# First pair's reads between its substitution's steps, three gate and three value buffers, and keys behind the corner transposition

## The chip, the cores and the metric

The kernel runs on one core of a Trainium2 chip. The metric is device time in microseconds (us). Three runs of the kernel before are shown, and their median is 1071.92 us. The engines are named as in the profile: PE multiplies matrices (PEld is its weight load), DVE is the vector engine, ACT the scalar engine, POOL a third elementwise engine, and SP issues nearly all DMAs, in order.

## The reference

One layer of a decoder trunk over 512 positions and 2048 channels, in float32:

```python
h = rms_norm(x, norm_g[i])
z = jnp.einsum('btd,dn->btn', h, w_in[i])          # 2048 -> 6272 columns
... token shift on r, k, v and two low-rank inputs
decay = jnp.exp(-jnp.exp(w_loglog)); a = jax.nn.sigmoid(a0[i] + ad @ a_up[i])
kk = kk / jnp.maximum(jnp.linalg.norm(kk, axis=-1, keepdims=True), KK_EPS)
def step(S, inp):                                  # 16 heads of 64, 512 steps
    sa = jnp.einsum('bhvk,bhk->bhv', S, -kk_t)
    S = S * w_t[:, :, None, :] + sa[..., None] * (kk_t * a_t)[:, :, None, :] + v_t[..., None] * k_t[:, :, None, :]
    return S, jnp.einsum('bhvk,bhk->bhv', S, r_t)
y_rwkv = (head_group_norm(y, ln_w[i], ln_b[i]) + bonus) * jax.nn.silu(g_rwkv)
y_pool = per-group linear map of (trailing means - token), scaled, * jax.nn.silu(g_pool)
x = x + jnp.einsum('btc,cd->btd', concat(y_rwkv, y_pool), w_out[i])
x = x + sigmoid(x @ w_pg[i] + b_pg[i]) * (p[i] @ w_ple[i])
return rms_norm(x, final_g)
```

## The kernel before

Every large product runs as three matmuls: each float32 operand is split into a high part (a cast on ACT, line 133 for weights) and a low part (a subtraction on DVE, line 134), and high·high, high·low and low·high are summed in PSUM (`mm3`). Weights come in chunks of 256 KB (`wsplit`): `raw` is loaded by SP, `whi` and `wlo` are made from it, and each of the three has four buffers. `chunk` asks for weights some six chunks ahead of their use.

The work on the 16 heads goes in eight pairs (`j` from 0 to 7), 128 channels each. The recurrence is worked out in chunks of 64 positions. For each pair:

- `prepare` makes the decayed queries `ar` and the keys `bk` (line 615 the half without the norm, line 619 the half with it), and stores `bk` to memory (`bkd`).
- `scores` multiplies them (`pm`), masks the result into `mt`, stores a part of it (`nd`), and reads it back as the factor of a triangular system, in two halves of four DMAs (`n_read(0)` and `n_read(1)`, line 682). The list `later` holds what else is to be read: the second half, the next pair's low-rank weights (`load_ab`, line 355), and the keys in blocks (`bg`, line 693, twice two DMAs).
- `invert` solves the system by substitution in 31 steps, two DVE instructions each (lines 719 and 723). The first 16 steps read the first half of the factor, the others the second. The result `xw` goes through memory (`xd`, line 727) to `x1` (line 734).
- `gather` transposes the corner block of `x1` (`y1`, line 789) and feeds it to PE (`pq2`, then `px2`) to complete the inverse. For the first two pairs the norm of the next pair's keys (line 572, `late`) is ordered ahead of that transposition. `turn_key` (line 639) transposes the keys that were read.
- `recur` goes over the eight chunks of positions, with the next pair's `scores` and `invert` between its hops; `finish`, `turn_out` and `gate_out` (lines 960 to 985) store the pair's output during the next pair, where line 979 adds the bonus and line 980 multiplies by the gate.

Between all this the kernel puts the projection's matmuls (`pump(n)` puts n of them; `stream` lists the column blocks: for each pair k, r, v, one or more blocks of the pool half, and the gate g). Their results are `sk`, `sr`, `sv` and `sg`; a gate is made from PSUM on ACT (line 374) and DVE (line 375). `psA`, their accumulators, has two buffers.

PE's instructions stay in program order in this part (`keep_in_program_order`). For the other engines the framework lays out an order before the run: it takes the earliest instruction in the program whose inputs and buffers it estimates to be ready. `tc.issue_after(i)` puts instructions behind `i` on its engine, and `tc.high_priority` ahead of others. On the chip each engine's order is fixed.

For the pairs from the second on, the entries of `later` wait in the list `portions`, and `recur` takes one out after each hop. For the first pair, which has no `recur` ahead of it, they were issued all at once behind `n_read(0)`:

```python
for fn in later if j == 0 else ():
    with tc.issue_after(n_.ins):
        fn()
portions[:] = [(n_, fn) for fn in later] if j else []
```

The first pair's substitution was driven by `for _ in invert(0): pump(4)`, that is 124 matmuls beside 31 steps.

Of the kernel before, what the change touches and what calls it, by code (L numbers as in the profile page):

```python
# [9 lines left out]
F32 = mybir.dt.float32  # L10
# [5 lines left out]
P = 128  # L16
# [18 lines left out]
def trunk_kernel(ctx: ExitStack, tc: tile.TileContext, x, p, norm_g, w_in, mu, w0, w_up, a0, a_up,  # L35
# [426 lines left out]
    def stream():  # L462
        for kind, nm, j in jobs:
            if kind == "b":
                yield from pool_unit(j)
                continue
            if kind == "e":
                yield from embed_unit(j)
                continue
            if kind == "p":  # L470
                for k in range(2):
                    pt = rw.tile([P, T], F32, name=f"ppt{k}", tag=("kk", "kp")[k])
                    nc.vector.transpose(pt.rearrange("p (b k) -> p b k", k=32), pn[0][:, k])
                    a_ = rw.tile([P, T], F32R, name=f"phi{k}", tag=("sk", "sr")[k], bufs=2)
                    b_ = rw.tile([P, T], F32R, name=f"plo{k}", tag=("sv", "sg")[k], bufs=(4, 2)[k])
                    split(a_, b_, pt)
                    phl.append((a_, b_))
                yield 3
                continue
            ps = psA.tile([P, T], F32, name=f"z{nm}{j}", tag="acc")  # L480
            yield from zcols(ps, f"{nm}{j}")
            t_ = rw.tile([P, T], F32, name=f"s{nm}{j}", tag=f"s{nm}", bufs=4 if nm == "v" else 2)
            if nm == "g":
                silu2(ps, t_)
            else:
                shifted(ps, t_, {"r": 0, "k": 8, "v": 16}[nm] + j)
            zt[nm, j] = t_
# [24 lines left out]
                assert (nm, j) in zt  # L512
        return zt[nm, j]

    pws, kks, nrs, vgs, late = {}, {}, {}, {}, [None]

    H1, H2, H3, H4, H5, HE = 6, 12, 20, 8, 13, 40

# [79 lines left out]
    def prepare(j):  # L598
        k_, r_, v_ = need("k", j), need("r", j), need("v", j)
        pw, ipw, tha = pws.pop(j)  # L600
        kk = kks.pop(j)


        ar = rw.tile([P, NCH // 2, 4, C], F32, name=f"ar{j}", tag="ar", bufs=2)
        bk = rw.tile([P, NCH // 2, 4, C], F32, name=f"bk{j}", tag="bk")
        k4 = kk.rearrange("p (q c t) -> p q c t", c=2, t=C)
        pw4 = pw.rearrange("p (q c) t -> p q c t", c=2)
        i4 = ipw.rearrange("p (q c) t -> p q c t", c=2)
        kp = rw.tile([P, T], F32, name=f"kp{j}", tag="kp")
        nc.vector.tensor_scalar(kp, tha, dp(33, j), dp(41, j), ALU.mult, ALU.add)  # L610
        nc.vector.tensor_tensor(kp, kp, k_, ALU.mult)
        nc.vector.tensor_scalar(tha, tha, 0.5, 0.5, ALU.mult, ALU.add)
        nc.vector.tensor_tensor(ar[:, :, 0::3, :], r_.rearrange("p (q c t) -> p q c t", c=2, t=C),
                                pw4[:, :, :, 1:C + 1], ALU.mult)
        nc.vector.tensor_tensor(bk[:, :, 0::3, :], kp.rearrange("p (q c t) -> p q c t", c=2, t=C), i4, ALU.mult)
        nc.vector.scalar_tensor_tensor(ar[:, :, 1:3, :], k_.rearrange("p (q c t) -> p q c t", c=2, t=C), dp(89, j),
                                       pw4[:, :, :, 0:C], ALU.mult, ALU.mult)
        nc.vector.tensor_tensor(kk, kk, tha, ALU.mult)
        made = nc.vector.tensor_tensor(bk[:, :, 1:3, :], k4, i4, ALU.mult)
        with tc.issue_after(made.ins):  # L620
            nc.vector.scalar_tensor_tensor(kp, r_, dp(49, j), kp, ALU.mult, ALU.mult)
        kph = rw.tile([P, T], F32R, name=f"kph{j}", tag="t", bufs=4)
        kpl = rw.tile([P, T], F32R, name=f"kpl{j}", tag="t", bufs=4)
        split(kph, kpl, kp)

        if j:
            vd = dram.tile([P, T], F32, name=f"vd{j}", tag="vd")
            with tc.issue_after(read[-1].ins):
                nc.sync.dma_start(out=vd, in_=v_)
            vgs[j] = rw.tile([P, NT, 4, 32], F32, name=f"vg{j}", tag="t", bufs=4), vd  # L630
        bkd = dram.tile([P, NCH * P], F32, name=f"bkd{j}", tag="bkd")
        nc.sync.dma_start(out=bkd, in_=bk.rearrange("p q s c -> p (q s c)"))
        st_[j] = dict(pw=pw, ar=ar, bk=bk, bkd=bkd, v_=v_, kp=(kph, kpl))
# [8 lines left out]
    def scores(j):  # L642
        ar, bk, v_ = (st_[j][n_] for n_ in ("ar", "bk", "v_"))
        kph, kpl = st_[j].pop("kp")

        mt = rw.tile([P, 2, 8, 2, C], F32, name=f"mt{j}", tag="mt", bufs=2)
        pm = [[psM.tile([P, T], F32, name=f"pm{j}_{par}0", tag="m"),
               psY.tile([P, T], F32, name=f"pm{j}_{par}1", tag="y")] for par in range(2)]
        for par in range(2):
            for q in range(4):  # L650
                for h in range(2):
                    rows = slice(64 * h, 64 * h + 64)
                    mm(pm[par][h][:, q * P:(q + 1) * P], bk[rows, q, 2 * par:2 * par + 2, :],
                       ar[rows, q, 2 * par:2 * par + 2, :], start=True, stop=True)
        for par in range(2):
            for h in range(2):
                nc.vector.tensor_tensor(mt[:, par, h::2, :, :],
                                        pm[par][h].rearrange("p (u a t) -> p u a t", u=4, a=2),
                                        msk[:, par:par + 2, :].unsqueeze(1).to_broadcast([P, 4, 2, C]), ALU.mult)


        ps = psM.tile([P, T], F32, name=f"pbo{j}", tag="m")
        mm(ps, blk, kph, start=True, stop=False)
        mm(ps, blk, kpl, start=False, stop=True)
        bv = v_ if j else rw.tile([P, T], F32, name=f"bv{j}", tag="sv", bufs=4)
        nc.vector.tensor_tensor(bv, ps, v_, ALU.mult)

        nd = dram.tile([2, 2, 8, 32, 32], F32, name=f"nd{j}", tag="nd")
        for par in range(2):
            pb = 64 * (1 - par)  # L670
            for b in range(2):
                rows = slice(pb + 32 * b, pb + 32 * b + 32)
                nc.sync.dma_start(out=nd[par, b].rearrange("u r c -> r u c"),
                                  in_=mt[rows, par, :, 1 - par, 32 * b:32 * b + 32])
        nb = []
        for i in range(2):
            t_ = rw.tile([P, 16, 32], F32, name=f"n32{j}_{i}", tag=("kk", "kp")[i])
            nb.append(t_)

        def n_read(i):  # L680
            for q in range(4):
                r_ = nc.sync.dma_start(out=nb[i][32 * q:32 * q + 32], in_=nd[:, :, :, 16 * i:16 * i + 16, :].rearrange(
                    "a b u r c -> (a b u) r c"))
            return r_

        n_ = n_read(0)
        if j:
            hold[:] = [n_]
        bg = rw.tile([P, NCH, 4, 32], F32, name=f"bg{j}", tag="bk")

        def blocks(dst, src, qs):
            for q in qs:
                nc.sync.dma_start(out=dst[32 * q:32 * q + 32],
                                  in_=src.rearrange("(b k) (c q i) -> q k c b i", b=4, q=4, i=32)[q])

        later = [lambda: n_read(1)]
        if j + 1 < NJ:
            later.append(lambda: load_ab(j + 1))
        for qs in ((0, 1), (2, 3)):
            later.append(lambda qs=qs: blocks(bg, st_[j]["bkd"], qs))  # L700
        if j:
            vg, vd = vgs[j]
            for qs in ((0, 1), (2, 3)):
                later.append(lambda qs=qs: blocks(vg, vd, qs))
        for fn in later if j == 0 else ():
            with tc.issue_after(n_.ins):
                fn()
        portions[:] = [(n_, fn) for fn in later] if j else []
        st_[j].update(mt=mt, nb=nb, bv=bv, bg=bg)


# [30 lines left out]
    def gather(j):  # L742
# [44 lines left out]

        with tc.issue_after(late[0].ins):
            yt = nc.vector.transpose(y1, x1[:, :, 0:32])
        with tc.issue_after(yt.ins):  # L790
            if normed:
                normed.pop()()
                stores.pop()()
            if j + 1 < NJ:
                scale_key(j + 1)
# [27 lines left out]
        if gates:  # L823
            gates.append(gates.pop()())


    def recur(j, work, between):
        d = st_.pop(j)
# [16 lines left out]
        for ch in range(NCH):  # L845
# [67 lines left out]
                        yr = slice(64 * pr, 64 * pr + 64)  # L913
                        nc.scalar.copy(ysb[yr, c0 // 2:c0 // 2 + 2, :], py4[yr, pr::2, :])
            step()
            if portions:
                n_, fn = portions.pop(0)
                with tc.issue_after(n_.ins):
                    fn()
            if ch == 1 and gates:  # L920
                with tc.issue_after(lead[0].ins):
                    gates.pop()()
# [77 lines left out]
    pump(H3)  # L1000
    scores(0)
    pump(H2)
    for _ in invert(0):
        pump(4)
    pump(HT - 124)
    gather(0)
# [319 lines left out]
```

## Time and profile before

| | |
|---|---|
| three runs | 1071.4, 1072.0 and 1071.92 us |
| the profiled execution | 1071.41 us, span 1069.7 us |
| granted clock of PE, mean | 0.995 |
| PE busy | 1042.4 us (97%) |
| DVE busy | 713.2 us (67%) |
| ACT busy | 433.5 us (41%) |

The span is the time from the first to the last instruction, and the run's time includes what lies around it. The pairs take the stretch from about 60 to 690 us. Times in the views are us from the span's start; a row of a time line has start, duration, engine, line, operation, output and inputs, and in brackets how long the engine had been idle and what ended that.

### The profile page before, as it was taken

The numbers are of one execution on the slowest core, as the hardware profiler recorded it, in microseconds if no ns is written. First come the engines' busy times: TensorE is split into PE (matmuls) and PEld (weight loads), VectorE is DVE, ScalarE is ACT, GpSimd is POOL, SyncE is SP. The second block draws the span as 40 slices with busy tenths as digits, with TensorE's granted clock in tenths as the row PEclk, the third lists the DMA queues.
The fourth block names the chain that finished last, engine by engine and source line by source line (L and its number), as shares of the span: only waits on it lengthen the run. The fifth ranks groups of instructions, "written<-read, shape, count | busy, mean of one in ns | idle before, by whom it ended". The sixth has DMA issues, their size and how long they took to land.

```text
span 1069.7 us, 17217 instructions
## 1 busy us (share of the span) xinstructions
PE 1042.4 (97%) x5884; PEld 862.0 (81%) x5884; DVE 713.2 (67%) x1878; ACT 433.5 (41%) x893; POOL 75.7 (7%) x180
## 2 busy tenths in 40 slices
PE   5998999999999999999999999999999999999996
PEld 4886888888888888887888888888888888888885
DVE  6677768978788788797787868454444344436356
ACT  7633424434334344353343345543222232323337
POOL 2100011010110110201101101000000000000000
PEclk9999999999999999999999999999999999999998
DMA  7444443553544645535446454774847659455434
GB/s 238 106 120 97 130 126 92 149 146 95 159 117 129 171 103 149 139 93 155 115 118 181 106 139 132 252 233 160 202 143 178 166 149 262 133 185 169 158 99 157
DMA packets 292174, 159.08 MB, mean 149 GB/s; under 512 B 130306, under 2 KB 254827, under 8 KB 292087
## 3 DMA queue, kind: packets, MB, share of 16 engines
q1 hardware_dynamic: 264070, 129.41, 44.3%
q10 hardware_dynamic: 28016, 28.58, 8.8%
q8 instruction: 46, 0.75, 0.3%
q14 instruction: 42, 0.34, 0.1%
HBM read 130.63 MB, written 26.79 MB: 147 GB/s over the span
## 4 chain that ended last, share of the span: by engine, by line
PE 93%; DVE 3%; ACT 2%; DMA 1%; issue 1%; SPq 0%; ACTq 0%; DVEq 0%
PE acc_o L161 16%; PE acc_g L161 16%; PE zb L161 16%; PE zv L161 8%; PE zg L161 8%; PE zr L161 8%; PE zk L161 7%; PE pple L161 2%; PE py L161 2%; PE pu L161 2%; PE pm L161 1%; PE ps L161 1%; PE pp L161 1%; PE pmv L161 1%; PE zl L161 1%; ACT hhi L287 1%
## 5 line engine op out<-in xcount | busy, mean ns | idle before, releaser
L134 DVE TENSOR_TENSOR wlo_g<-raw_g,whi_g 128x512 fp32r<-128x512 f32 x84 | 57.2, 688 | 81.7 <-ACT whi_g L133 81.6
L161 PE MATMUL zb<-hhi,whi_b 128*128 128x512 f32 x256 | 105.1, 411 | 0.0
L161 PE MATMUL zb<-hhi,wlo_b 128*128 128x512 f32 x256 | 100.3, 392 | 0.0
L161 PE MATMUL zb<-hlo,whi_b 128*128 128x512 f32 x256 | 99.8, 390 | 0.0
L161 PE MATMUL acc_o<-wlo_o,yhi 128*128 128x512 f32 x256 | 99.6, 389 | 0.0
L161 PE MATMUL acc_o<-whi_o,ylo 128*128 128x512 f32 x256 | 99.6, 389 | 0.0
L134 DVE TENSOR_TENSOR wlo_o<-raw_o,whi_o 128x512 fp32r<-128x512 f32 x64 | 43.8, 690 | 80.3 <-ACT whi_o L133 80.1
L133 ACT CAST whi_g<-raw_g 128x512 fp32r<-128x512 f32 x84 | 51.8, 619 | 106.9 <-PE acc_g L161 52.6
L161 PE MATMUL acc_o<-whi_o,yhi 128*128 128x512 f32 x256 | 94.7, 389 | 0.0
L161 PE MATMUL acc_g<-whi_g,x2hi 128*128 128x512 f32 x208 | 81.2, 390 | 0.0
L161 PE MATMUL acc_g<-wlo_g,x2hi 128*128 128x512 f32 x208 | 80.9, 389 | 0.0
L899 POOL TENSOR_SCALAR s0p<-sbd,pw 64x64 f32<-64x64 f32 x96 | 57.8, 602 | 325.1 <-DVE sbd L892 247.0
L161 PE MATMUL acc_g<-whi_g,x2lo 128*128 128x512 f32 x208 | 80.7, 390 | 0.0
L133 ACT CAST whi_o<-raw_o 128x512 fp32r<-128x512 f32 x64 | 39.5, 621 | 95.2 <-PE acc_o L161 58.3
L133 ACT CAST whi_b<-raw_b 128x512 fp32r<-128x512 f32 x64 | 39.5, 620 | 55.3 <-PE zv L161 17.5
L134 DVE TENSOR_TENSOR wlo_b<-raw_b,whi_b 128x512 fp32r<-128x512 f32 x64 | 43.9, 688 | 22.9 <-ACT whi_b L133 22.1
L161 PEld LDWEIGHTS zb<-hhi,wlo_b 128*128 128x128 f32 x256 | 48.0, 188 | 10.8
L723 DVE TENSOR_TENSOR xw<-xw,tm 128x60 f32<-128x60 f32 (+24 forms) x248 | 52.1, 210 | 6.8
L161 PEld LDWEIGHTS acc_o<-wlo_o,yhi 128*128 128x128 f32 x256 | 48.1, 188 | 10.1
L161 PEld LDWEIGHTS acc_o<-whi_o,yhi 128*128 128x128 f32 x256 | 48.0, 188 | 10.0
L161 PEld LDWEIGHTS acc_o<-whi_o,ylo 128*128 128x128 f32 x256 | 48.0, 188 | 9.9
L161 PE MATMUL zr<-hhi,whi_r 128*128 128x512 f32 x128 | 53.9, 421 | 1.3 <-DVE sg L375 1.3
(293 smaller groups left out, 2490.0 us busy)
## 6 DMA issues: line engine op xcount, KB each, us to landing
raw_b<-in_w_in_dram SPq DMA_DIRECT2D x64, 256.0 KB
raw_o<-in_w_out_dram SPq DMA_DIRECT2D x64, 256.0 KB
raw_g<-in_w_pg_dram SPq DMA_DIRECT2D x64, 256.0 KB
raw_k<-in_w_in_dram SPq DMA_DIRECT2D x32, 256.0 KB
raw_r<-in_w_in_dram SPq DMA_DIRECT2D x32, 256.0 KB
raw_v<-in_w_in_dram SPq DMA_DIRECT2D x32, 256.0 KB
raw_g<-in_w_in_dram SPq DMA_DIRECT2D x32, 256.0 KB
bkd<-bk SPq DMA_DIRECT2D x8, 512.0 KB
```

Of the source, the lines that this page charges most:

```text
L133: made.append(nc.scalar.copy(hi, raw))
L134: made.append(nc.vector.tensor_tensor(lo, raw, hi.bitcast(F32), ALU.subtract))
L161: i = nc.tensor.matmul(*a, **k)
L287: nc.scalar.activation(hhi[:, d, hc], pt[:, 0:256], AF.Copy, scale=ngc[:, d:d + 1])
L723: nc.vector.tensor_tensor(xw[:, 0:n_, s + 1:32], xw[:, 0:n_, s + 1:32], tm[:, 0:n_, 0:w_], ALU.add)
L899: nc.gpsimd.tensor_scalar(s0p[hc, :], nxt[hc, hc], pcn[hc], None, ALU.mult)
```

## The change

Four edits. The first pair's reads go into the same list `portions` as those of the later pairs, and `next_read` takes one out behind the 3rd, 7th, 11th and 14th step of its substitution (`s` is 2, 6, 10 and 13); the order behind `n_read(0)` stays. The gates `sg` get three buffers in place of two, and the values `sv` three in place of four; the two tiles of the embedding (`plo`) that share these buffers follow. The first key product of a pair (line 615) is ordered behind the corner transposition of the pair before it; the first pair has none.

```diff
-                    b_ = rw.tile([P, T], F32R, name=f"plo{k}", tag=("sv", "sg")[k], bufs=(4, 2)[k])
+                    b_ = rw.tile([P, T], F32R, name=f"plo{k}", tag=("sv", "sg")[k], bufs=3)
...
-            t_ = rw.tile([P, T], F32, name=f"s{nm}{j}", tag=f"s{nm}", bufs=4 if nm == "v" else 2)
+            t_ = rw.tile([P, T], F32, name=f"s{nm}{j}", tag=f"s{nm}", bufs=3 if nm in "vg" else 2)
...
-        nc.vector.tensor_tensor(bk[:, :, 0::3, :], kp.rearrange("p (q c t) -> p q c t", c=2, t=C), i4, ALU.mult)
+        with tc.issue_after(corner[0].ins) if corner else ExitStack():
+            nc.vector.tensor_tensor(bk[:, :, 0::3, :], kp.rearrange("p (q c t) -> p q c t", c=2, t=C), i4, ALU.mult)
...
-        bv = v_ if j else rw.tile([P, T], F32, name=f"bv{j}", tag="sv", bufs=4)
+        bv = v_ if j else rw.tile([P, T], F32, name=f"bv{j}", tag="sv", bufs=3)
...
-        for fn in later if j == 0 else ():
-            with tc.issue_after(n_.ins):
-                fn()
-        portions[:] = [(n_, fn) for fn in later] if j else []
+        portions[:] = [(n_, fn) for fn in later]
...
             yt = nc.vector.transpose(y1, x1[:, :, 0:32])
+        corner[:] = [yt]
...
+    def next_read():
+        if portions:
+            n_, fn = portions.pop(0)
+            with tc.issue_after(n_.ins):
+                fn()
...
-            if portions:
-                n_, fn = portions.pop(0)
-                with tc.issue_after(n_.ins):
-                    fn()
+            next_read()
...
-    for _ in invert(0):
+    for s, _ in enumerate(invert(0)):
+        if s in (2, 6, 10, 13):
+            next_read()
         pump(4)
```

More of the change, by code (lines that the diff above doesn't have):

```diff
@@ L513, in need @@
         return zt[nm, j]
-    pws, kks, nrs, vgs, late = {}, {}, {}, {}, [None]
+    pws, kks, nrs, vgs, late, corner = {}, {}, {}, {}, [None], []
     H1, H2, H3, H4, H5, HE = 6, 12, 20, 8, 13, 40
```

## The prediction

> **What bounds the kernel now.** I began with the page's span and busy lines.
>
> ```profile
> span 1069.7 us, 17217 instructions
> ...
> PE 1042.4 (97%) x5884; PEld 862.0 (81%) x5884; DVE 713.2 (67%) x1878; ACT 433.5 (41%) x893; POOL 75.7 (7%) x180
> ```
>
> TensorE is busy for 97% of the span, so an edit that removes no matmul can win only where PE stands still, or where its clock drops after it stood still. The second view is therefore the waits of PE alone (total us, times, longest), and the third the stretches of 2 us around the longest wait past the start-up.
>
> ```profile
> PE zr L161 <- DVE wlo_r L134: 4.0, 1, 4.0
> ...
> PE zr L161 <- DVE sg L375: 1.3, 1, 1.3
> PE pq L161 <- DVE y L789: 0.8, 1, 0.8
> ...
> PE pu L161 <- DVE zs L859: 0.4, 1, 0.4
> ```
>
> ```profile
> 104.00:106.00 2.00, 0.00 (x0) 0.00 (x0) 1.86 (x7) 0.00 (x0) 0.00 (x0) 1.00 0.00 0
> ...
> 108.00:110.00 2.00, 2.00 (x6) 1.51 (x6) 0.63 (x2) 0.00 (x0) 0.00 (x0) 0.50 0.92 267
> 110.00:112.00 2.00, 2.00 (x8) 1.55 (x7) 0.88 (x2) 1.21 (x2) 0.00 (x0) 0.73 0.91 231
> ```
>
> Past the start-up four waits of PE stand in the list. Three touch what the diff edits: weights during the first pair's substitution, a gate (sg), and the corner transposition (y). The stretches (busy PE, PEld, DVE, ACT, POOL, then PE clock, DMA share, GB/s) add that the longest wait costs more than its 4.0 us: behind it the granted clock is 0.50 and 0.73 in two stretches. The DMA share is zero from 104 to 106, so PE waits for no transfer there, while DVE works 1.86 of 2 us.
>
> **Part 1: the first pair's reads in portions.** The time lines of PE, DVE, ACT and SP (start, duration, engine) tell how the wait comes about.
>
> ```profile
> 98.65 0.39 PE L161 MATMUL zr<-hhi,wlo_r 128*128 128x512 f32 x1
> 102.50 0.39 PE L161 MATMUL zr<-hlo,whi_r 128*128 128x512 f32 x1
> 106.88 0.50 PE L161 MATMUL zr<-hhi,wlo_r 128*128 128x512 f32 x1 [3.99 <-DVE wlo_r L134]
> 111.08 0.39 PE L161 MATMUL zv<-hlo,whi_v 128*128 128x512 f32 x1
> 83.91 0.69 DVE L134 TENSOR_TENSOR wlo_k<-raw_k,whi_k 128x512 fp32r<-128x512 f32 x1 [2.03 <-ACT whi_k L133]
> 104.94 1.31 DVE L639 STREAM_TRANSPOSE bkn<-bg 128x512 f32<-128x512 f32 x2
> 106.17 0.65 DVE L134 TENSOR_TENSOR wlo_r<-raw_r,whi_r 128x512 fp32r<-128x512 f32 x1
> 106.74 1.88 DVE L134 TENSOR_TENSOR wlo_v<-raw_v,whi_v 128x512 fp32r<-128x512 f32 x3
> 98.31 0.62 ACT L133 CAST whi_r<-raw_r 128x512 fp32r<-128x512 f32 x1
> 82.48 3.61 SPq L682 DMA_DIRECT2D n<-nd  x8
> 88.63 3.18 SPq L693 DMA_DIRECT2D bg<-bkd  x4
> 91.91 0.62 SPq L130 DMA_DIRECT2D raw_r<-in_w_in_dram  x1
> ```
>
> The matmul at 106.88 needs the low half of r's fourth weight chunk. Its high half was done on ACT at 98.31 + 0.62 = 98.93, but DVE's order has the low half behind the whole substitution and both key transpositions, which begin where it ends (104.94). The chunk had been loaded late: its buffer was free once wlo_k ended at 83.91 + 0.69 = 84.60, and its load was issued at 91.91, because from 82.48 to 91.81 SP issued the eight reads of the factor, four of the low-rank weights and four of the keys in a row. An order laid out for a chunk that comes late puts its split late.
>
> The price: the 18 rows of zr from 98.65 to 102.50 have 17 spacings, 0.2265 us each. From 102.50 to 111.08 there are 12 spacings, 2.72 us at that pace, and 8.58 passed. The loss is **5.86 us**: 4.15 of standing, and 1.71 at the low clock.
>
> After the edit 12 of these reads go behind steps 2, 6, 10 and 13 of the substitution, so SP can take the r and v loads between. No DMA is added. The next pair's reads go in portions already, with two weight loads between the halves of the factor:
>
> ```profile
> 145.20 1.71 SPq L682 DMA_DIRECT2D n<-nd  x4
> 146.95 0.98 SPq L130 DMA_DIRECT2D raw_k<-in_w_in_dram  x2
> 147.97 1.90 SPq L682 DMA_DIRECT2D n<-nd  x4
> ```
>
> In that pair's substitution PE has no wait for weights in the list above, so I take the whole 5.86 as the gain. Cover: the fourth r load can go some 6 us sooner (about 86 instead of 91.91), which leaves its split 16 us before 102.5.
>
> What is late next? DVE is nearly full in the stretch from 104 above. The four splits at 106.17 and 106.74 (0.65 + 1.88, say 2.5 us) move into the substitution, whose end goes from 104.94 to about 107.4. Behind it hangs the way of its result through memory to the corner transposition y, and from there PE's pq:
>
> ```profile
> 107.45 1.57 SPq L130 DMA_DIRECT2D raw_b<-in_w_in_dram  x3
> 109.07 2.07 SPq L727 DMA_DIRECT2D xd<-xw  x3
> ...
> 120.89 0.43 DVE L789 STREAM_TRANSPOSE y<-x 128x256 f32<-128x256 f32 x1
> 125.77 0.69 PE L161 MATMUL pq<-y,mt 32*32 32x32 f32 x32
> ...
> 470.17 2.53 SPq L727 DMA_DIRECT2D xd<-xw  x4
> 474.63 2.87 SPq L734 DMA_DIRECT2D x<-xd  x4
> ```
>
> PE will want pq at 125.77 − 5.86 = 119.9. Where no weight loads stand between, as at 470.17, the way takes 7.33 us to the last read's issue, and about 1.9 more to land (472.70 to 474.63 is that for the write): 107.4 + 9.3 + 0.43 = 117.1, 2.8 before PE asks. Where loads stand ahead of the stores, as the three at 107.45 do now, y slips by the whole 2.5 and ends at 123.8, and PE waits 3.9, with a clock loss of up to 1.7. So the give-back lies between 0 and 5.6; below nothing it could go by the 0.4 that PE now waits for zs, if a new order heals that. I take **0.4**: the small waits of the seven later pairs (1.3 + 0.8 + 0.4 over 7) are the nearest rows of a pair with portions. The low-rank weights load later too, but nothing reads them before the matmuls that stand behind the whole substitution in PE's order.
>
> What would a remnant at pq cost? The wait of 3.99 lost 1.71 by the clock, 0.43 for each us; in proportion a remnant of 2.5 us would cost 3.6. The Trainium skill, "TensorE: Matmul & The Clock Gate", Part 1, says otherwise: the array falls to half rate only after an idle window of about 3.4 us. By that rule such a remnant costs its own 2.5 us, and the first rival below would give 1066.5 rather than 1067.5. The trace agrees so far: behind the wait of 1.35 at 508 the clock stays at 1.00.
>
> ```profile
> 506.00:510.00 4.00, 2.65 (x13) 2.07 (x12) 3.50 (x8) 1.68 (x3) 0.90 (x2) 1.00 0.90 268
> ```
>
> **Part 2: three gates, three values.** The seventh gate's activation waits for a buffer.
>
> ```profile
> 507.44 0.60 ACT L374 ACTIVATE sg<-zg 128x512 f32<-128x512 f32 x1 [2.72 <-DVE yo L980]
> 508.81 0.50 PE L161 MATMUL zr<-hhi,whi_r 128*128 128x512 f32 x1 [1.35 <-DVE sg L375]
> ...
>   ACT sg L374: 8.0, 3
> ```
>
> With two buffers, gate j+2 waits until gate j is multiplied in at line 980 (8.0 us of ACT in three pairs, by the view of the tile sg); once PE has filled its other accumulator it stands too. A third buffer takes that release away. Gain 1.35 plus the 0.16 by which the first wait's standing exceeded its idle time (4.15 against 3.99): **1.51 us**. The other two waits are beside PE and bring nothing. The values pay with one of four buffers.
>
> ```profile
> 219.52 0.69 DVE L979 TENSOR_TENSOR yo<-yo,bv 128x512 f32<-128x512 f32 x1
> 260.08 0.69 ACT L370 ACTIVATE sv<-zv,dprm 128x512 f32<-128x512 f32 x1
> ```
>
> The first pair's bonus (bv) is last read at 219.52 + 0.69, and the value that with three buffers takes its place (the fourth pair's) is written at 260.08. That cover is 40 us, so the edit costs nothing; without it the value would wait for line 979 as the gate does for 980.
>
> **Part 3: keys behind the corner transposition.**
>
> ```profile
> 481.00 0.68 DVE L615 TENSOR_TENSOR bk<-kp,ipw 128x512 f32<-128x512 f32 x1
> 483.15 0.43 DVE L789 STREAM_TRANSPOSE y<-x 128x256 f32<-128x256 f32 x1
> ```
>
> The key product stands ahead of y on DVE, and this y is the one that PE waits 0.8 for in the list of waits. y's input had been fetched long before (issues end at 474.63 + 2.87 = 477.50), so y comes earlier by what is taken out: at most the 0.68 of that row, of a loss of 0.8 + 0.16 = 0.96. Instructions on DVE start a little before the one ahead has ended (106.17 + 0.65 against 106.74), so I take **0.60**. The wait that is added is on DVE; behind the key product only the store of both halves of the keys is queued, and the other half still waits for its norms, so it costs nothing. If that cover were gone, it would be the same 0.60 on the way to the scores.
>
> **The sum.** 5.86 − 0.4 + 1.51 + 0.60 = 7.57 us. The profiled execution took 1071.41 us (span 1069.7 and 1.7 around it), 0.5 under the median of the runs shown, 1071.92. So it would take 1063.84, and a run of median kind **1064.3 us**.
>
> **The rivals.**
> *The wait moves to pq.* The result of the substitution keeps its place behind weight loads, and PE waits there 1 to 3.9 us. For it: DVE is full and SP is in order. Against it: loads that go out earlier no longer stand between. Gain 7.97 − (1 to 5.6): 1065 to 1069.5.
> *The portions change nothing.* Order on SP and DVE is laid out by estimated readiness; if the fourth r split stays behind line 639, only parts 2 and 3 are left: 1071.92 − 2.1 = 1069.8. Against it: by the rows above it was a late load that put the split there, and nothing else.
>
> ```profile
> 97.23 0.23 DVE L719 TENSOR_TENSOR tm<-xw,n 128x75 f32<-128x75 f32 x1
> ```
>
> *Slower: a portion comes too late.* DVE is in order. If the second factor half or the last keys are queued on SP behind loads that wait for buffers, DVE stands at step 17 or at line 639, with the splits behind it. A wait W there is added to today's stall: 1071.92 − 2.1 + W, slower by 0.2% from W = 4.3. The 17th step, the first to read the second half, begins at 97.23 now, so that half would have to land after 101.5. Against it: its reads are issued by 82.48 + 3.61 = 86.09 now, and would have to slip by a dozen us, past several loads, though their place is behind step 2 of 31. Time at W = 6: 1075.8.
>
> **How the numbers follow.** A measurement of this kernel tells from no change about 0.2%, 2.1 us. Forecast 0.63 (its own range 1062.6 to 1066), moved wait 0.17, no effect of the portions 0.11, late portion 0.09. All of the first two cases but 0.01, and half of the third, are faster: 0.84. Same: 0.08. Slower: 0.08, most of the fourth case. The range reaches from 1062.6 (everything gained, and the 0.4 healed) to 1069.8, the third case.
>
> **What would show it.** Right: no wait of PE for wlo_r, clock 1.00 in every stretch between 100 and 112, raw_r loads between the n and bg reads on SP, no row of ACT sg waiting for line 980, line 615 behind line 789 in every pair but the first. Wrong: a wait of PE at pq near 118, a DVE row of the substitution that waits for nb's or bg's transfer, or new waits for weights in later pairs, where everything is laid out anew.

## The result: 0.6% faster, and the profile after

| | before | after |
|---|---|---|
| median of five runs | 1071.92 us | 1066.03 us |
| range | 1071.4 to 1072.54 | 1065.28 to 1066.23 |
| the profiled execution | 1071.41, span 1069.7 | 1066.03, span 1064.3 |
| granted clock of PE, mean | 0.995 | 0.997 |

The ratio is 0.994, with a 95% interval of 0.9929 to 0.9951. Further down a run stands as such a ratio against runs of the kernel before on the same chip; a few disturbed executions (2120 us and more) are left out of the ratios.

The waits of PE in the changed kernel, those of the start-up left out (total us, times, longest):

```profile
PE pq L161 <- DVE y L787: 1.5, 2, 1.1
PE pu L161 <- DVE zs L864: 0.9, 3, 0.4
```

The waits for wlo_r (4.0) and for the gate sg (1.3) are gone. The wait for y, at 0.8 before, is now 1.5 in two places (0.4 in the first pair, 1.1 in the sixth), and that for zs (a tile of the recurrence), one of 0.4 before, is 0.9 in three. The stretches of 2 us where PE had stood show it busy throughout, at full clock (third number from the end):

```profile
104.00:106.00 2.00, 2.00 (x10) 1.65 (x10) 1.76 (x9) 0.40 (x1) 0.00 (x0) 1.00 0.07 16
108.00:110.00 2.00, 2.00 (x11) 1.65 (x10) 2.00 (x5) 0.62 (x1) 0.00 (x0) 1.00 0.10 16
110.00:112.00 2.00, 2.00 (x13) 1.67 (x12) 0.87 (x3) 1.19 (x2) 0.00 (x0) 1.00 0.73 216
```

The time line of SP in the changed kernel shows what the portions did to the queue:

```profile
82.89 3.61 SPq L683 DMA_DIRECT2D n<-nd  x8
86.54 1.12 SPq L355 DMA_DIRECT2D ur<-in_w_up_dram  x2
87.71 1.23 SPq L355 DMA_DIRECT2D ar<-in_a_up_dram  x2
89.04 0.53 SPq L130 DMA_DIRECT2D raw_r<-in_w_in_dram  x1
89.67 0.45 SPq L130 DMA_DIRECT2D raw_v<-in_w_in_dram  x1
90.22 1.40 SPq L694 DMA_DIRECT2D bg<-bkd  x2
...
110.28 1.87 SPq L725 DMA_DIRECT2D xd<-xw  x3
112.26 2.40 SPq L130 DMA_DIRECT2D raw_g<-in_w_in_dram  x2
114.84 1.85 SPq L732 DMA_DIRECT2D x<-xd  x4
```

In the columns of a time line (start, duration, engine, line, operation, output and input, count), both halves of the factor and the low-rank weights still go out in one row, although in the program they are portions of their own, behind the 3rd and the 7th step. Only the keys (bg) moved behind the fourth r load, which left at 89.04 and not at 91.91. And loads of g still stand between the stores of the substitution's result and its reads.

DVE and ACT answer with another order. The fourth r chunk's high half is made at 94.49 in place of 98.31, and its low half inside the substitution (rows of ACT, then of DVE):

```profile
94.49 0.62 ACT L133 CAST whi_r<-raw_r 128x512 fp32r<-128x512 f32 x1 [1.38 <-PE zk L161]
95.94 0.69 DVE L134 TENSOR_TENSOR wlo_r<-raw_r,whi_r 128x512 fp32r<-128x512 f32 x1
99.33 0.69 DVE L134 TENSOR_TENSOR wlo_v<-raw_v,whi_v 128x512 fp32r<-128x512 f32 x1
107.37 1.29 DVE L640 STREAM_TRANSPOSE bkn<-bg 128x512 f32<-128x512 f32 x2
...
119.50 0.75 DVE L371 SCALAR_TENSOR_TENSOR sv<-zv,prm,sv 128x511 f32<-128x511 f32 x1
120.17 0.44 DVE L787 STREAM_TRANSPOSE y<-x 128x256 f32<-128x256 f32 x1
```

### The profile page after: what moved, and what is told of

Read it like the earlier page. It is cut to its first block, busy times and chain, and to the rows that moved or that the text cites. A ratio compares the mean times of both kernels' runs of the same rounds, so it can differ in the third digit from the quotient of the medians.

```text
span 1064.3 us, 17220 instructions
## 1 busy us (share of the span) xinstructions
PE 1040.8 (98%) x5884; PEld 861.4 (81%) x5884; DVE 714.1 (67%) x1878; ACT 434.0 (41%) x893; POOL 75.6 (7%) x180
## 4 chain that ended last, share of the span: by engine, by line
PE 84%; DVE 3%; issue 1%; ACT 0%; DMA 0%; ACTq 0%; DVEq 0%
PE acc_o L161 16%; PE acc_g L161 16%; PE zb L161 14%; PE zg L161 7%; PE zv L161 6%; PE zr L161 6%; PE zk L161 6%; PE pple L161 2%; PE py L161 2%; PE pu L161 2%; PE pm L161 1%; PE ps L161 1%; PE pp L161 1%; PE pmv L161 1%; DVE sw L418 1%
## 5 line engine op out<-in xcount | busy, mean ns | idle before, releaser
L878 ACT COPY uv<-pu 64x64 f32<-64x64 f32 x128 | 26.3, 205 | 73.4 <-PE pu L161 72.4
```

The source lines that it names most:

```text
L878: u_ = nc.scalar.copy(uv[pb:pb + 64, ch, hc], psu[hc, hc])
```

## The experiments

Four questions: do the edits add up, and which of them pays; was the load of r late, or only DVE's order; what does the low clock cost; and what makes the waits for y. The first edit is here that of the reads, the second that of both kinds of buffers (gates and values), the third that of the key product. In the quoted expectations "the prediction's step" is the one above.

### One edit at a time

The first edit alone:

> The first edit alone (the first pair's reads in portions). Theory: the 4.0 us wait of PE for wlo_r and the 1.71 us at low clock go, and the wait of 0.4 for y at the first pair comes, so 5.86 - 0.60 = 5.3 us: 1066.6. The waits of PE for sg (1.3) and for y in the sixth pair (0.8) stay as before. Rival: the gain of the three edits does not split, because every order is laid out anew; then this run is off 1066.6 by over 1 us, and the waits for sg and y are others than before.

Measured 0.9948 (0.9934 to 0.9961). PE's waits in its profile:

```profile
PE zr L161 <- DVE sg L375: 1.4, 1, 1.4
PE pq L161 <- DVE y L786: 1.2, 2, 0.8
PE acc_g L161 <- DVE gt L1193: 0.7, 1, 0.7
PE pu L161 <- DVE zs L862: 0.6, 2, 0.4
```

The wait for wlo_r is gone, a second one for y (0.4) has come, and those for sg and for the sixth pair's y (0.8) stand as before. A wait of 0.7 for gt (a tile of the layer's last stage), near 1013, is new and is not in the changed kernel. Of the 5.9 us of the whole change this edit brings some 5.6.

The second edit alone:

> The second edit alone (three gates, three values). Theory: the wait of PE for sg (1.35, with the refill 1.5) goes and nothing else: 1070.4, and the first pair's 4.0 us wait stays. Rival: the gate's wait was cover for something late behind it, which PE then waits for: 1071.9, with a new wait near 509.

Measured 0.9991 (0.9983 to 1.0), about 1.0 us less. In its profile the wait of 4.0 for wlo_r and that of 0.8 for y stay, and none for sg is left. But "nothing else" does not hold: two short waits are new, for zs (0.25, at 654) and for gt (0.25, at 1017), which take back a part of the gain. The interval holds the 1.5 expected, and reaches to no change, so for this edit the view of waits says more than the clock.

The third edit alone:

> The third edit alone (line 615 behind the corner transposition). Prediction's step: y 0.60 us sooner, 1071.3. Theory after the result: another instruction (line 422, 0.65) takes the place that line 615 leaves ahead of y, so PE's wait for y in the sixth pair is 0.8 to 1.1 and the time 1071.9 to 1072.3.

Measured 1.0003 (0.9993 to 1.0012). PE's wait for y is 1.1. DVE's order ahead of the sixth pair's y in this kernel:

```profile
480.62 0.75 DVE L617 SCALAR_TENSOR_TENSOR ar<-sk,dprm,pw 128x512 f32<-128x512 f32 x1
...
482.43 0.69 DVE L422 SCALAR_TENSOR_TENSOR u<-sw,u 128x512 f32<-128x512 f32 x1
483.04 0.44 DVE L790 STREAM_TRANSPOSE y<-x 128x256 f32<-128x256 f32 x1
```

Line 615 is no longer there, but line 422, which used to come behind y, now comes ahead of it.

All but the third edit:

> All edits but the third. If the third edit brings nothing or costs 0.3, as the wait for y of 1.1 in place of 0.8 says, this is 1065.5 to 1066.0. If the third edit brings the 0.60 somewhere else, this is 1066.6.

Measured 0.9944 (0.9932 to 0.9957), the same as the changed kernel. Its wait for the sixth pair's y is 0.8, and not 1.1. The third edit brings nothing that can be measured.

### Which reads have to move

```diff
-        portions[:] = [(n_, fn) for fn in later]
+        for fn in later[:2] if j == 0 else ():
+            with tc.issue_after(n_.ins):
+                fn()
+        portions[:] = [(n_, fn) for fn in (later if j else later[2:])]
...
-        if s in (2, 6, 10, 13):
+        if s in (10, 13):
```

> Only the keys' reads (bg) go in portions, behind the 11th and 14th step; the factor's second half and the low-rank weights are issued at once as before. Theory after the result: in the changed kernel's trace these two still stand in one row behind the first half, so only the keys' move counts, and this equals the first edit alone: no wait for wlo_r, about 5.3 us less than before (1066.6 to 1067). Rival, the prediction's step: all twelve reads have to be spread; then a part of the 5.3 is missing.

Measured 0.9945 (0.9933 to 0.9958), as the first edit alone. Moving the keys' four reads is the whole of it.

```diff
-        if s in (2, 6, 10, 13):
-            next_read()
+        for _ in range(4 if s == 2 else 0):
+            next_read()
```

> The first edit, but all four portions behind the third step. Theory: the place of the keys' reads among the loads decides; here they go out ahead of the fourth r load again, so the wait of 4.0 us for wlo_r and the low clock come back: same as before. Rival: that the reads come from the list, behind the matmuls, is enough: 5.3 us less.

Measured 0.9998 (0.9989 to 1.0007): no change. On SP the keys go ahead of the r load again:

```profile
88.51 3.05 SPq L693 DMA_DIRECT2D bg<-bkd  x4
91.66 0.62 SPq L130 DMA_DIRECT2D raw_r<-in_w_in_dram  x1
```

PE's wait of 4.0 for wlo_r is back. So it is their place that counts, and not that they come from the list.

### A late load, or only a late place in DVE's order

The kernel before, with its reads as they were. `lows` holds each chunk's low-half instruction:

```diff
+    FORCED = {20: ('r1', 3)}
...
+            with tc.issue_after(lows[FORCED[s]].ins) if j == 0 and s in FORCED else ExitStack():
                 nc.vector.tensor_tensor(tm[:, 0:n_, 0:w_], ...
```

> The kernel before with its reads at once, but DVE's order changed: the 21st step of the first pair's substitution is ordered behind the low half of r's fourth chunk (wlo_r). Theory: the load was there in time (its high half was made at 98.31, and PE asks at 102.5) and DVE's order alone cost the 5.86 us; then wlo_r is done by about 101.8, PE does not wait, and about 5.3 us go without any change to the reads. Rival: the load or the full DVE is late; then DVE stands ahead of the 21st step, and PE waits for 2 us or more at wlo_r or at the v chunks behind it.

Measured 0.9936 (0.9923 to 0.9948). SP's row is the old one, and DVE does the low half in time, behind the two key transpositions, which now stand inside the substitution too. SP's time line, then DVE's:

```profile
88.21 3.15 SPq L694 DMA_DIRECT2D bg<-bkd  x4
91.46 0.62 SPq L130 DMA_DIRECT2D raw_r<-in_w_in_dram  x1
```

```profile
99.33 1.30 DVE L640 STREAM_TRANSPOSE bkn<-bg 128x512 f32<-128x512 f32 x2
100.56 0.65 DVE L134 TENSOR_TENSOR wlo_r<-raw_r,whi_r 128x512 fp32r<-128x512 f32 x1
101.26 0.68 DVE L134 TENSOR_TENSOR wlo_v<-raw_v,whi_v 128x512 fp32r<-128x512 f32 x1
```

PE has no wait for wlo_r, and none for y in the first pair; one of 1.5 for gt, near 1012, is new. So the load was not late for PE in the kernel before either, and its place in SP's order mattered only through DVE's order. That DVE's order was laid out for a chunk that was thought to come later fits all these runs, but the framework's estimates themselves are in no trace.

### What the low clock adds

The prediction cites a rule of the Trainium skill ("TensorE: Matmul & The Clock Gate", Part 1) by which the clock falls only behind an idle window of about 3.4 us. The same order, but ahead of the 29th step and of the 27th (`FORCED = {28: ...}` and `{26: ...}`), makes the wait shorter.

> As the kernel with the low half ahead of the 21st step, but ahead of the 29th: wlo_r ends near 105.6, and PE stands about 3.0 us instead of 4.0. If the low clock behind the wait of 4.0 comes only from an idle time of over about 3.4 us, the clock stays at 1.00 and the loss is 3.2, that is 2.7 us less than before. If the clock loss goes with the length of the wait (0.43 per us), the loss is 4.3 and only 1.6 us go.

> As the kernel with the low half ahead of the 29th step, but ahead of the 27th, so that PE stands about 1.8 us (2.73 there, and the clock still fell for 1.73 us of loss). If the clock falls for every wait of about 2 us, the loss is 3.7 and 2.1 go against before; if it falls only for longer ones, the loss is 2.0 and 3.9 go.

Rows of PE, first of the kernel with step 29, then of that with step 27:

```profile
103.36 0.39 PE L161 MATMUL zr<-hlo,whi_r 128*128 128x512 f32 x1
106.47 0.50 PE L161 MATMUL zr<-hhi,wlo_r 128*128 128x512 f32 x1 [2.73 <-DVE wlo_r L134]
107.56 0.63 PE L161 MATMUL zr<-hhi,whi_r 128*128 128x512 f32 x1
110.92 0.39 PE L161 MATMUL zv<-hhi,wlo_v 128*128 128x512 f32 x1
```

```profile
102.36 0.39 PE L161 MATMUL zr<-hlo,whi_r 128*128 128x512 f32 x1
104.55 0.50 PE L161 MATMUL zr<-hhi,wlo_r 128*128 128x512 f32 x1 [1.80 <-DVE wlo_r L134]
107.40 0.39 PE L161 MATMUL zv<-hhi,wlo_v 128*128 128x512 f32 x1
```

With step 29, 13 spacings took 7.56 us in place of 2.94 (13 x 0.2265): a loss of 4.62, of which 2.88 is standing (3.11 less one spacing) and 1.73 the low clock with the refill. With step 27, 13 spacings took 5.04: a loss of 2.10, of which 1.96 is standing, and the clock stays at 1.00. The 0.14 left is the refill: the first spacing behind a wait is longer (104.55 to 104.89 in that trace) at full clock too. So the low clock by itself costs some 1.6, here and in the kernel before, where 1.71 was put down to it. The ratios agree in kind: 0.9983 (0.9974 to 0.9992), some 1.8 us less than before, and 0.996 (0.9946 to 0.9973), some 4.3 less.

So the threshold of 3.4 us does not hold for the trace with step 29: the clock drops already after 2.73 of idle time. A price by length comes near its time, but gives 1.2 there where 1.73 was lost, and 0.8 at step 27, where only the refill was. What fits these traces is a fall that comes or not, at 1.7 us with the refill, behind 2.73 but not behind 1.80. That the length of the wait alone decides is not shown. The trace with step 29 is of the slowest of its eleven executions. The two fastest (1069.36 and 1069.84) had a mean clock of 0.998, as kernels without a fall have, and which no execution in the ratios reached where the wait was 4.0; so the clock probably did not fall in these two.

### The waits for y, and a faster version

> The changed kernel once more, to stand beside the next two on the same chip: 5.9 us less than before, PE's waits for y 0.4 and 1.1.

Measured 0.9941 (0.9929 to 0.9954), with y's waits of 0.4 and 1.1.

```diff
             yt = nc.vector.transpose(y1, x1[:, :, 0:32])
         corner[:] = [yt]
+        if j == 0:
+            follow(moved[-1], yt)
+            follow(lows["b0", 3], yt)
+        if j == 5:
+            follow(sums[-1], yt)
```

`follow(i, of)` puts instruction `i` behind `of` on its engine; `moved` holds the shifts of line 371, `sums` the window sums of line 418.

> The changed kernel with the corner transposition y put ahead on DVE by two explicit orders: in the first pair the shift of v and the last low half of b stand behind it, in the sixth the second window sum (line 418) and so line 422. Theory: y's data are there, and only what DVE's order has ahead of it makes PE wait; then both waits for y go (0.60 and 1.22 with refill): 1.8 us less than the changed kernel. Rival: the data come late (x's reads from memory); then y starts no sooner and the waits stay.

Measured 0.9926 (0.9913 to 0.9938), some 1.6 us under the changed kernel beside it, by ratios whose intervals overlap. PE has no wait for y left. On DVE, first and sixth pair:

```profile
118.29 0.45 DVE L793 STREAM_TRANSPOSE y<-x 128x256 f32<-128x256 f32 x1 [0.44 <-DMA x<-xd]
...
476.59 0.44 DVE L793 STREAM_TRANSPOSE y<-x 128x256 f32<-128x256 f32 x1
476.96 0.65 DVE L424 TENSOR_TENSOR sw<-sw 128x510 f32<-128x510 f32 x1
```

In the first pair y now starts when its data land, 118.29, where it had stood at 120.17 behind other work; in the sixth at 476.59, where it had stood at 478.40 behind line 422, as these rows of the changed kernel show:

```profile
477.79 0.69 DVE L422 SCALAR_TENSOR_TENSOR u<-sw,u 128x512 f32<-128x512 f32 x1
478.40 0.44 DVE L787 STREAM_TRANSPOSE y<-x 128x256 f32<-128x256 f32 x1
```

The data were there, and the order was the cause, in both places.

> A candidate: the kernel before with its reads at once, the low half of r's fourth chunk ahead of the 21st step of the first pair's substitution, the second edit (three gates, three values), and the sixth pair's y ahead of the second window sum. Theory: 5.86 + 1.5 + about 0.8 less than before: 1063.8, with no wait of PE over 0.5 us past the start-up. Rival: without the portions the three do not add up; over 1065.5.

Measured 0.9921 (0.9908 to 0.9935), by median 1064.38 beside 1066.51 for the changed kernel. Its waits of PE past the start-up are one row:

```profile
PE pu L165 <- DVE zs L869: 0.7, 2, 0.4
```

So a kernel that leaves the reads as they were and writes two places of DVE's order by hand, with the gates' third buffer, is faster than before and, by medians on one chip, than the change (the two intervals overlap). It and the kernel with y ahead can't be told apart.

## Why the prediction was right, and where it was not

The direction, the place and the main term held; the gain of the medians is 5.9 us in place of 7.6. The median, 1066.03, lies just outside the forecast's own range (1062.6 to 1066), whose lower end is also about 1 us below what the named gains give with the 0.4 healed (5.86 + 1.51 + 0.60 + 0.4 = 8.37, and 1071.92 − 8.37 = 1063.55). Term by term, by the starts of PE's matmuls in the two profiled executions:

- *First pair, 5.86:* right. No wait, no low clock in that stretch, and 5.6 us by the ratio of the edit alone, a small give-back included. The step that named the cause was right in kind: an order laid out for a late chunk. But that 12 reads would go between the loads was wrong: eight of them did not move, and the four of the keys did it all. The fourth r load went out 2.9 us sooner, and not some 6, and that was enough.
- *Give-back at pq, 0.4:* the place was right, and the size near by luck: 0.4 was a mean of later pairs' waits, most of them of another kind. The wait is 0.43, and PE loses 0.50 there beside the kernel before (0.82 from the matmul ahead of pq to pq, in place of 0.32). My reckoning had the data landing at 116.7 where no loads stand between; loads of g do, and they landed at 118.3, as the kernel with y ahead shows. The rest, to 120.17, is DVE's order and was not foreseen.
- *Gates, 1.51:* right in the trace. The loss (1.6: from 507.08 to 508.81 between two matmuls, where the changed kernel takes 0.14) is gone with the edit and stays without it. By the measured time of the edit alone the gain is 1.0, with an interval from 0 to 1.8; the two short waits that came with it take a part.
- *Corner, 0.60:* wrong in sign. PE's loss there went from 0.95 to 1.22, so the term is −0.27. The step that failed is "y comes earlier by what is taken out". It took DVE's order for a row of which one piece can be drawn out, while the order is laid out anew: line 615 went, and line 422 came ahead of y. That the framework's estimate of when y's data land did this is likely, and not shown.
- *Start-up and later pairs:* not foreseen, and small. The first matmul waited 7.2 in place of 6.8 in the profiled run, and two waits for zs are new:

```profile
602.10 0.49 PE L161 MATMUL pu<-zs,x 128*128 128x128 f32 x2 [0.22 <-DVE zs L864]
648.70 0.49 PE L161 MATMUL pu<-zs,x 128*128 128x128 f32 x2 [0.25 <-DVE zs L864]
```

Each costs some 0.5 with the refill. The first is there with the first edit alone, the second with the second edit alone. With the terms above (5.86 − 0.50 + 1.6 − 0.27 − 0.4 − 1.0) that makes 5.3; the span went down by 5.4.

Of the rivals, *the wait moves to pq* came true in small: 0.43 us, and not 1 to 3.9. *The portions change nothing* is what the kernel with all portions behind the third step shows; the outcome hung on where the keys' reads stood. No portion came too late. The Trainium skill's rule on the clock, which the prediction weighed, does not hold here with its 3.4 us: in the traces an idle time of 2.73 was enough, and 1.80 was not. A remnant of 2.5 us at pq might well have cost the clock too.

## What to carry to other kernels

Where PE waits for an instruction of another engine whose inputs are long there, suspect the order of that engine: here an explicit order that put the instruction ahead gave the whole gain of the first edit, and no transfer had to move. Taking a piece of work away from ahead of a late instruction need not bring it forward where the order is laid out anew: here something else filled the place. What must not stand ahead is better ordered behind it. And test an edit of several parts one part at a time: here one gave nearly all, one about 1 us, and one nothing.

## What was not expected of the hardware

In the traces the granted clock of PE fell to 0.50 behind idle times of 2.73 us and of 4.0, and not behind 1.80 or 1.35. In all five traces with a fall it stayed low for 3.4 us: from 104 to 113 the mean clock is 0.81 in each, that is 3.4 of 9 us at half. So the price of some 1.6 us was the same behind 2.73 us of waiting as behind 3.99. The moment of the fall was not tied to PE's restart. It came about 1 us behind it with step 29 (restart at 106.47, slow spacings from 107.56), and with the third edit alone the clock was low already when PE restarted:

```profile
106.56 0.80 PE L161 MATMUL zr<-hhi,wlo_r 128*128 128x512 f32 x1 [4.01 <-DVE wlo_r L134]
107.15 0.63 PE L161 MATMUL zr<-hhi,whi_r 128*128 128x512 f32 x1
```

What sets the moment and the 3.4 us was not tried, nor whether a wait of 2.7 us always brings a fall.
